# A sparse-attention decoder step: the samples' top-256 search as eight rows with halvings on ScalarE, and two prompt blocks halved on ScalarE alone

## The chip, the cores and the metric

The kernel runs on one core of a Trainium2 chip. The metric is the device time of one execution in microseconds (us); the time before is the median of three runs. A profile was taken of one further execution; its times are counted from the start of its span.

## The reference, cut to what matters

One layer of a hybrid decoder: a projection of the normalised input into many column groups, sparse attention on one branch, a causal pooling mixer on the other, and an output projection. The change touches the choice of the keys in the sparse attention. For every query the indexer gives a score per key, and only the 256 keys with the largest scores are attended to:

```python
s = jnp.einsum('bqhd,bld->bqhl', qi, ki)
score = jnp.einsum('bqh,bqhl->bql', wi, jax.nn.relu(s))
score = jnp.where(causal[None], score, -jnp.inf)
_, sel = lax.top_k(score, topk)          # topk = 256
```

The prompt has 1024 queries, in eight blocks of 128; blocks 0 and 1 have at most 256 keys and need no choice, block b has (b + 1) * 128 keys. There are eight sample sequences with one query each, over 1024 cached keys and the sample's own.

## The kernel before

The kernel keeps x transposed, makes the modulated input h as eight pairs of row tiles (an upper and a lower half, 16 tiles), and projects it for 21 column groups. A group's product goes in three chunks of 344 columns, 24 products of TensorE each (three for every k of 8). After every second k the function `project` calls `tick`, so a tick is six products, a chunk has four and a group twelve. Every other step of the kernel is a generator in a named queue, and a tick lets each queue's first generator go one step on, times its rate: a queue with rate 0.5 goes on at every second tick. TensorE, VectorE and ScalarE run their instructions in the order in which the code gives them out; so a side product whose input is late stops the projection behind it. GpSimd's order and the slots of tiles are left to the scheduler.

After the prompt's scores are made (`indexer`), 13 groups follow in the order u0 u1 u2 gp0 u3 gp1 q0 gp2 q1 gp3 q2 q3 ga3; ticks are counted here from the first product of u0 (184.19 us in the trace), so gp2 begins at tick 84. Beside them run:

- queue "smp", rate 1: `sample_indexer` (scores of the samples into s_sc, 128 partitions by 9 by 8: eight key slots and the own key, eight samples), then `sample_topk` from tick 49. It splits the scores into 16-bit halves and finds the 256th value by trying seven candidates at once, in twelve rounds: compare on VectorE (L968), count by nine products with ones on TensorE (`total`, L954, after five more ticks), choose on VectorE. Two more counts and a ranking of equal values follow, and the masks s_m.
- queue "top", rate TOP = 0.5: `topk` for the prompt's six blocks. Eight halvings of a threshold t by counting: blocks 7, 6, 5 by a Sign with accumulator on ScalarE (L758), 4, 3, 2 by a comparison with accumulator on VectorE (L761); then three tiny VectorE steps on all six (L764, L766, L768) make the next t, for which all six counts wait. Two steps (yields) a halving. After them those at or over t are marked (L773, L778), the at most 16 still missing are taken in two rounds of eight largest (L792) and replacement (L799); if that doesn't do, a branch runs 30 more rounds. The masks follow.
- queue "prep": among others `windows(g)` for the pooling group g, begun after u_g: GpSimd makes one to four running sums (L1187, with a copy of the edge columns, L1188), three ticks apart, VectorE's step follows (L1192 to L1197), then ScalarE casts the upper half pdh (L1201), GpSimd makes the lower half pdl (L1202) and TensorE turns the last columns (put, L1204). For g = 3 the first sum is given out at tick 61, VectorE's step at 73, the cast at 74.
- queue "pool": `take_gp` multiplies the pooled halves by w_pool on TensorE (ppo, L1217) for each chunk of gp_g; the last product of group 1 is given out at tick 75.
- queue "weights": the next group's weights, loaded two groups ahead, split one group ahead into an upper half on ScalarE (L293) and a lower half on GpSimd (L297), at the group's third tick.

Row tiles (up to 4 KB on each partition) come from one pool of 29. When group 3's first sum is given out, these 27 are taken: 16 of h, 5 of scores, up_out, pdh and pdl of groups 1 and 2, u3, and the sum itself would be one more, a second sum beside it the 29th.

Of the kernel before, what the change touches and what calls it, by code (L numbers as in the profile page):

```python
# [21 lines left out]
TOP = 0.5  # L22
# [8 lines left out]
LAG = 5  # L31
# [34 lines left out]
def kernel(  # L66
# [634 lines left out]
    def ordered_halves(hi, lo, src, sign):  # L701
        v = src.bitcast(I16).rearrange("p (n t) -> p n t", t=2)
        nc.vector.tensor_copy(hi, v[:, :, 1])
        nc.vector.tensor_copy(lo, v[:, :, 0].bitcast(U16))
        yield
        nc.vector.tensor_scalar(sign, hi, 0.0, -1.0, op0=ALU.is_lt, op1=ALU.mult)
        nc.vector.tensor_tensor(lo, lo, sign.bitcast(U16), op=ALU.bitwise_xor)
        yield
        nc.vector.scalar_tensor_tensor(hi, sign, 0x7FFF, hi, op0=ALU.bitwise_and, op1=ALU.bitwise_xor)

    TB = (7, 6, 5, 4, 3, 2)
    BY_ACT = (7, 6, 5)
    NT = len(TB)
# [12 lines left out]
    tk_flag = const.tile([P, NT], BF16, name="tk_flag")  # L726
    for i, b in enumerate(TB):
# [7 lines left out]
    def width(i):  # L735
        return (TB[i] + 1) * P

    def topk():
# [13 lines left out]
        nc.vector.tensor_tensor(t, t, tk_mv[:, :, 0], op=ALU.add)  # L752
        for k in range(HALVINGS):

            for i, b in enumerate(TB):
                L = width(i)
                if b in BY_ACT:
                    nc.scalar.activation(junk_tile("sg", tag="junka", bufs=1)[:, :L], score[b], AF.Sign, scale=-1.0,  # L758
                                         bias=t[:, i:i + 1], accum_out=cnt[:, i:i + 1])
                else:  # L760
                    nc.vector.tensor_scalar(junk_tile("junk")[:, :L], score[b], t[:, i:i + 1], None,  # L761
                                            op0=ALU.is_lt, op1=ALU.add, accum_out=cnt[:, i:i + 1])
            yield
            nc.vector.tensor_tensor(tk["keep"], cnt, tk["least"], op=ALU.is_le)  # L764

            nc.vector.scalar_tensor_tensor(tk["d"], tk["keep"], 0.5 if k < HALVINGS - 1 else 0.0, tk_step[:, k],  # L766
                                           op0=ALU.subtract, op1=ALU.mult)
            nc.vector.tensor_tensor(t, t, tk["d"], op=ALU.add)  # L768
            yield
# [32 lines left out]
        yield  # L802
        for r in range(WINDOW // 8):
# [3 lines left out]
            if r == 0:  # L807
                pb = ps_side("p_bad", (P, NT))
                mm(pb, ones_b, tk_flag, start=True, stop=True)
            those(r)  # L810
            if r == 0:
                yield
                with nc.allow_low_precision(reason="a count of at most 768"):
                    nc.vector.tensor_reduce(out=tk_bad, in_=pb[0:1, :], axis=AX.X, op=ALU.add)
# [3 lines left out]
        with tc.If(nc.vector.value_load(tk_bad) != 0, preferred_fallthrough_block=False):  # L818
            for r in range(WINDOW // 8, TOPK // 8):
# [44 lines left out]

    def s_bc(t):
        return t.unsqueeze(1).to_broadcast([P, 9, B])

    def sample_indexer():
# [54 lines left out]
        def weigh(b):  # L923
# [8 lines left out]
    steps = const.tile([P, 7, B], F32, name="steps")  # L932
    nc.gpsimd.iota(steps, pattern=[[1, 7], [0, B]], base=1, channel_multiplier=0,
                   allow_small_or_imprecise_dtypes=True)

    def sample_topk():
        s_hi = const.tile([P, 9 * B], I16, name="s_hi")
        s_lo = const.tile([P, 9 * B], U16, name="s_lo")
        s_sg = const.tile([P, 9 * B], I16, name="s_sg")
        nc.vector.tensor_scalar(s_sc, s_sc, 0.0, None, op0=ALU.add)  # L940
        yield from ordered_halves(s_hi, s_lo, s_sc.rearrange("p g b -> p (g b)"), s_sg)
        s_hi, s_lo = (t.rearrange("p (g b) -> p g b", b=B) for t in (s_hi, s_lo))
        s_H, s_low, s_ngt, s_least, s_need = (const.tile([P, B], F32, name=f"s_{n}")
                                              for n in ("H", "low", "ngt", "least", "need"))
        s_gt = const.tile([P, 9, B], BF16, name="s_gt")
        s_eq = const.tile([P, 9, B], BF16, name="s_eq")

        def total(flags, n):

            for _ in range(LAG):  # L950
                yield
            pt = ps_side("p_cnt", (P, n))
            for g in range(9):
                mm(pt, ones_b, flags[:, g], start=g == 0, stop=g == 8)  # L954
            yield
            return pt
# [806 lines left out]
```

## Time and profile before

| | us |
|---|---|
| time before, median of 3 runs (lowest to highest) | 648.01 (647.17 to 648.94) |
| the profiled execution | 648.84 |
| its span, first to last instruction | 647.1 |
| TensorE busy | 608.4 |
| VectorE busy | 403.9 |
| ScalarE busy | 291.1 |
| GpSimd busy | 256.9 |

TensorE is named PE in the rows, VectorE DVE, ScalarE ACT, GpSimd POOL. A busy time is the union of an engine's instructions; matmuls are pipelined and their ends are modelled, so 0.32 us of a product stands in the rows where the next one starts 0.16 us later. "PEclk" is the TensorE clock that was granted, as a share of the full one. Idle time is told with what ended it ("<- engine tile line"). Row lists by engine and time begin with start and duration in us.

### The profile page before, as it was taken

The page shows a single profiled execution, that of the slowest core. Times are in us where ns is not written, and L with a number is a line of the kernel's source. Part 1 is how long each engine was busy: PE and PEld are TensorE (multiplying, and loading weights), DVE is VectorE, ACT ScalarE, POOL GpSimd, SP SyncE. Part 2 cuts the span into 40 slices and gives each one's busy share as a digit, 9 for nine tenths or more (in the row PEclk, how much of TensorE's full clock was granted, in tenths as well). Part 3 has the DMA queues.
Part 4 walks back from the last instruction along what each step waited for, and adds up shares of the span by engine and source line. Part 5 has one row for each costly group of instructions (what it writes and reads, how often), then busy time and mean ns, then how long its engine had stood idle before and what let it go on. Part 6 is the DMA issues. An engine that isn't in the chain of part 4 may idle for free.

```text
span 647.1 us, 10990 instructions
## 1 busy us (share of the span) xinstructions
PE 608.4 (94%) x4197; PEld 500.5 (77%) x4197; DVE 403.9 (62%) x918; ACT 291.1 (45%) x518; POOL 256.9 (40%) x237
## 2 busy tenths in 40 slices
PE   5798998999989978979999988999999999999997
PEld 5587988999979868978988875656675666878876
DVE  4676364736467779997775546565687755554242
ACT  5634444444547865231222545755687544202000
POOL 3586434111267556552543690610445143106000
PEclk9999999999999988997999997999999999999999
DMA  8993115031245122121454250321221036146322
GB/s 304 297 291 61 50 44 152 16 84 55 76 128 147 34 66 56 44 58 44 99 135 138 89 164 26 138 99 33 66 67 34 1 99 220 43 151 209 98 97 68
DMA packets 75292, 66.05 MB, mean 102 GB/s; under 512 B 21828, under 2 KB 63900, under 8 KB 75229
## 3 DMA queue, kind: packets, MB, share of 16 engines
q1 hardware_dynamic: 69731, 50.57, 27.5%
q0 software_dynamic: 3008, 10.49, 5.3%
q10 hardware_dynamic: 2498, 4.27, 1.8%
q8 instruction: 33, 0.54, 0.3%
q14 instruction: 22, 0.18, 0.1%
HBM read 54.44 MB, written 11.10 MB: 101 GB/s over the span
## 4 chain that ended last, share of the span: by engine, by line
PE 74%; DVE 13%; ACT 5%; POOL 4%; DMA 2%; issue 2%; SPq 0%; POOLq 0%; ACTq 0%; DVEq 0%
PE py L1696 14%; PE po L1612 7%; PE pj_q L514 6%; PE pl L1575 6%; PE pT L1596 6%; PE pj_ga L514 5%; PE pj_qi L514 4%; PE pj_gp L514 4%; ACT sg L758 4%; PE pi L668 4%; PE pj_k L514 2%; PE pj_v L514 2%; DVE tk_t L768 2%; PE pj_u L514 2%; DMA vn<-in_cache_v_dram,pidx 1%
## 5 line engine op out<-in xcount | busy, mean ns | idle before, releaser
L1584 ACT ACTIVATE pr<-pr,mx,rq 128x128 f32<-128x128 f32 (+7 forms) x64 | 55.4, 866 | 18.2 <-DVE mx L1582 17.8
L677 DVE SCALAR_TENSOR_TENSOR sc<-r,wtok,sc 128x512 f32<-128x512 f32 (+5 forms) x42 | 44.1, 1060 | 27.9 <-ACT r L670 26.5
L670 ACT ACTIVATE r<-pi 128x512 f32<-128x512 f32 (+5 forms) x48 | 36.3, 759 | 54.1 <-PE pi L668 41.0
L1612 PE MATMUL po<-pTs,v_sb 128*64 128x256 f32 (+1 forms) x320 | 52.6, 381 | 0.0
L1696 PE MATMUL py<-woh,mh 128*128 128x512 f32 (+1 forms) x136 | 52.3, 384 | 0.0
L1696 PE MATMUL py<-woh,ml 128*128 128x512 f32 (+1 forms) x136 | 51.9, 382 | 0.0
L1696 PE MATMUL py<-wol,mh 128*128 128x512 f32 (+1 forms) x136 | 51.8, 381 | 0.0
L1596 PE MATMUL pT<-ident,pr 128*128 128x128 f32 x288 | 49.4, 285 | 0.1
L1578 DVE CUSTOM_DVE_ANT_0 pr<-pl,amask 128x384 f32<-128x384 f32 (+5 forms) x48 | 42.2, 887 | 10.9 <-PE pl L1575 10.5
L1596 PEld LDWEIGHTS pT<-ident,pr 128*128 128x128 f32 x288 | 33.0, 143 | 18.0 <-issue 15.8
L145 ACT COPY pTs<-pT 128x512 f32<-128x512 f32 x40 | 23.2, 581 | 34.6 <-PE pT L1596 34.6
L1716 DVE TENSOR_TENSOR y<-py,gate_p 128x512 f32<-128x512 f32 (+1 forms) x17 | 11.2, 657 | 43.0 <-PE py L1696 43.0
L1440 POOL TENSOR_TENSOR wol<-wo,woh 128x1024 fp32r<-128x1024 f32 x8 | 19.5, 2446 | 36.9 <-ACT woh L1439 30.6
L514 PE MATMUL pj_u<-hh,wh_u 128*128 128x344 f32 x96 | 32.5, 339 | 1.6 <-ACT r L670 1.6
L514 PE MATMUL pj_gp<-hh,wh_gp 128*128 128x344 f32 x96 | 33.5, 349 | 0.0
L514 PE MATMUL pj_q<-hh,wh_q 128*128 128x344 f32 x96 | 33.1, 345 | 0.0
L147 DVE COPY pTs<-pT 128x512 f32<-128x512 f32 (+1 forms) x40 | 23.3, 582 | 15.3 <-PE pT L1596 12.3
L514 PE MATMUL pj_gp<-hh,wl_gp 128*128 128x344 f32 x96 | 31.9, 332 | 0.0
L514 PE MATMUL pj_gp<-hl,wh_gp 128*128 128x344 f32 x96 | 31.8, 331 | 0.0
L514 PE MATMUL pj_q<-hl,wh_q 128*128 128x344 f32 x96 | 31.7, 330 | 0.0
L514 PE MATMUL pj_q<-hh,wl_q 128*128 128x344 f32 x96 | 31.6, 329 | 0.0
L1612 PEld LDWEIGHTS po<-pTs,v_sb 128*64 128x64 f32 x320 | 18.0, 135 | 17.4 <-issue 9.4
(451 smaller groups left out, 1780.3 us busy)
## 6 DMA issues: line engine op xcount, KB each, us to landing
ada<-in_w_ada_dram SPq DMA_DIRECT2D x16, 512.0 KB, 6.9
x<-in_x_prompt_dram SPq DMA_DIRECT2D x8, 512.0 KB, 5.4
gate<-in_w_ada_dram SPq DMA_DIRECT2D x8, 512.0 KB, 3.5
mix<-mix_dram SPq DMA_DIRECT2D x8, 512.0 KB, 3.1
xr<-in_x_prompt_dram SPq DMA_DIRECT2D x15, 256.0 KB
out_dram<-y ACTq DMA_DIRECT2D x15, 256.0 KB, 3.4
mix_dram<-sga SPq DMA_DIRECT2D x12, 172.0 KB, 4.9
mix_dram<-sgp SPq DMA_DIRECT2D x12, 172.0 KB, 2.8
```

Of the source, the lines that this page charges most:

```text
L147: nc.vector.tensor_copy(out, in_)
L514: mm(pt[:m, :n], wt[:, k, :m], ht[k][:, c0:c0 + n], start=k == 0 and q == 0, stop=k == KT - 1 and q == 2)
L668: mm(pt[:, c, :n], lhs, kk[:, l0:l0 + n], start=kk is kih, stop=kk is kil)
L670: nc.scalar.activation(r[:, 0:L].rearrange("p (c n) -> p c n", c=nh), pt[:, 0:nh, :n], AF.Relu)
L677: nc.vector.scalar_tensor_tensor(sb[:, 0:L], r[:, 0:L], wtok[:, b, h:h + 1], sb[:, 0:L], op0=ALU.mult, op1=ALU.add)
L758: nc.scalar.activation(junk_tile("sg", tag="junka", bufs=1)[:, :L], score[b], AF.Sign, scale=-1.0, bias=t[:, i:i + 1], accum_out=cnt[:, i: ...
L1575: mm(pt[:, c, :n], qst[j][s][:, b * P:(b + 1) * P], ksst[s][w][:, l0:l0 + n], start=w == 0, stop=w == 1)
L1578: nc.vector.tensor_tensor_reduce(out=pr[:, 0:L].rearrange("p (c n) -> p c n", c=nh), in0=pt[:, 0:nh, :n], in1=amask[b].rearrange("p (c n) ...
L1584: exps.append(lambda: nc.scalar.activation(pr[:, 0:L], pr[:, 0:L], AF.Exp, scale=sc, bias=mx, accum_out=sums[j, m][:, bq, s:s + 1]))
L1596: nc.tensor.transpose(pt[:, s, bq * P:(bq + 1) * P], probs[j, 2 * m + bq, s][:, k * P:(k + 1) * P], ident)
L1612: mm(po[j, m][64 * s:64 * s + 64, 0, q0:], v_sb[:, k, 64 * s:64 * s + 64], pTs[j, m, k][:, s, q0:], start=k == 0, stop=k == nk - 1)
L1696: mm(pt[:, part], a[k][:, bs], w[:, part], start=k == ks[0] and q == 0, stop=k == ks[-1] and q == 2)
```

## The change

It does four things. The samples' scores are turned into eight rows, one for each sample, of 1024 keys and the own one (`sample_search`, in place of `sample_topk`, `ordered_halves` and `total`): four transposes twice, mean and variance of the first 256 keys, eight halvings with three ScalarE instructions each (`half_way`: the Sign with accumulator, a Sign of the count against a limit, a new t), and two rounds of eight largest on VectorE (`sample_round`). Their masks are turned back by eight transposes (`sample_masks`), which the queue "top" now runs after the branch; the branch's flag counts the samples too, and `topk` waits with its own rounds until the queue "smp" is empty. Two row tiles are taken, s_row for the scores (until the masks) and s_fl for flags (until the marks). In the prompt's halvings blocks 7 and 6 go through `half_way`, so that no VectorE step lies between two of their counts; block 5 moves to VectorE, whose three tiny steps act on four blocks. A halving has three yields, and TOP is 0.6.

```diff
-TOP = 0.5
+TOP = 0.6
-LAG = 5
-    BY_ACT = (7, 6, 5)
-    NT = len(TB)
+    BY_ACT = (7, 6)
+    NT, NA = len(TB), len(BY_ACT)
+    def half_way(sc, t, cnt, lim, sign, step, junk):
+
+        nc.scalar.activation(junk, sc, AF.Sign, scale=-1.0, bias=t, accum_out=cnt)
+        nc.scalar.activation(sign, cnt, AF.Sign, scale=-1.0, bias=lim)
+        nc.scalar.activation(t, sign, AF.Identity, scale=step, bias=t)
...
+        for k in range(HALVINGS):
+            nc.gpsimd.tensor_scalar(tk_step[:, k, 0:NA], tk_step[:, k, 0:NA], 0.5, None, op0=ALU.mult)
...
+            for i in range(max(NA, NT - NA)):
+                if i < NA:
+                    half_way(score[TB[i]], t[:, i:i + 1], cnt[:, i:i + 1], tk_lim[:, i:i + 1], tk_sign[:, i:i + 1],
+                             tk_step[:, k, i:i + 1], junk_tile("sg", tag="junka", bufs=1)[:, :width(i)])
+                if i < NT - NA:
+                    o = NA + i
+                    nc.vector.tensor_scalar(junk_tile("junk")[:, :width(o)], score[TB[o]], t[:, o:o + 1], None,
+                                            op0=ALU.is_lt, op1=ALU.add, accum_out=cnt[:, o:o + 1])
+                if i % 2:
+                    yield
...
         chosen(0)
         yield
+        while queues["smp"]["gens"]:
+            yield
...
+                sample_round(r)
+        yield from sample_masks()
...
+    def sample_round(r):
+        sr = s_row["scores"]
+        sel, off, top = s_tk["sel"][:, 0:8], s_tk["off"][:, 0:8], s_tk["top"]
+        nc.vector.tensor_scalar(sel, tk_order[0:B, 0:8], 8.0 * r, s_tk["need"], op0=ALU.add, op1=ALU.is_lt)
+        nc.vector.tensor_scalar(off, sel, 1.0, -NEG, op0=ALU.subtract, op1=ALU.mult)
+        nc.vector.max(top, sr)
+        nc.vector.tensor_tensor(top, top, sel, op=ALU.mult)
+        nc.vector.tensor_tensor(top, top, off, op=ALU.add)
+        nc.vector.match_replace(sr, top, sr, NEG)
+
+    def sample_search():
+        sr = s_row["scores"] = row("s_row")[0:B, 0:S + 1]
+        fl = row("s_fl", BF16)[0:B, 0:S + 1]
...
+        for g in range(2):
+            pt = ps_side(f"p_row{g}", (B, 4, P))
+            for i in range(4):
+                nc.tensor.transpose(pt[:, i, :], s_sc[:, 4 * g + i, :], ident)
+            yield
+            nc.vector.tensor_scalar(by_slot(sr)[:, 4 * g:4 * g + 4, :], pt, 0.0, None, op0=ALU.add)
+            yield
...
+        nc.gpsimd.tensor_tensor(s_tk["sd"], s_tk["mv"][:, 1:2], tk["half"][0:B, 0:1], op=ALU.pow)
+        for k in range(HALVINGS):
+            nc.gpsimd.tensor_scalar(s_tk["step"][:, k:k + 1], s_tk["sd"], spans[7][1] * 2.0 ** -(k + 1), None, op0=ALU.mult)
+        nc.gpsimd.tensor_scalar(t, s_tk["sd"], spans[7][0], s_tk["mv"][:, 0:1], op0=ALU.mult, op1=ALU.add)
+        yield from lag(3)
+        for k in range(HALVINGS):
+            half_way(sr, t, s_tk["cnt"], s_tk["lim"], s_tk["sign"], s_tk["step"][:, k:k + 1], fl)
+            yield
+            yield
+        nc.vector.tensor_tensor(t, t, s_tk["step"][:, HALVINGS - 1:], op=ALU.add)
+        nc.vector.tensor_scalar(fl, sr, t, None, op0=ALU.is_ge, op1=ALU.add, accum_out=ngt)
+        yield
+        nc.vector.tensor_scalar(d, ngt, float(TOPK), NEG, op0=ALU.is_lt, op1=ALU.mult)
+        nc.vector.scalar_tensor_tensor(sr, fl, d, sr, op0=ALU.mult, op1=ALU.add)
...
+        for r in range(WINDOW // 8):
+            yield
+            sample_round(r)
+
+    def sample_masks():
...
+        yield from lag(2)
+        pt = ps_side("p_smask", (P, 8, B))
+        for i in range(8):
+            nc.tensor.transpose(pt[:, i, :], by_slot(sr)[:, i, :], ident[0:B, 0:B])
+        yield
+        nc.vector.tensor_copy(s_m[:, 0:8, :], pt)
+        yield
...
-    beside("smp", sample_topk(), 1.0)
+    beside("smp", sample_search(), 1.0)
...
-    drain("prep", "pool", "top", "smp", "stack")
+    drain("prep", "pool", "smp", "top", "stack")
```

## Rows read from the trace of the kernel before

**Rows 1.** The page: the chain that ended last, share of the span by engine.

```profile
PE 74%; DVE 13%; ACT 5%; POOL 4%; DMA 2%; issue 2%; SPq 0%; POOLq 0%; ACTq 0%; DVEq 0%
```

**Rows 2.** Stretches: us; busy PE, PEld, DVE, ACT, POOL (instructions); PEclk; DMA share; GB/s.

```profile
184.00:253.00 69.00, 62.49 (x421) 56.93 (x422) 52.33 (x140) 45.17 (x85) 44.71 (x44) 0.95 0.35 98
253.00:300.00 47.00, 41.01 (x277) 39.60 (x276) 44.06 (x76) 10.92 (x21) 25.07 (x17) 0.93 0.22 55
300.00:385.00 85.00, 85.00 (x670) 77.35 (x669) 54.82 (x127) 29.33 (x54) 47.72 (x26) 1.00 0.41 116
385.00:400.00 15.00, 10.89 (x48) 7.33 (x45) 7.95 (x36) 7.64 (x19) 4.22 (x3) 0.66 0.05 18
```

**Rows 3.** What PE waited for: us in total, times, longest us.

```profile
PE p_cnt L954 <- DVE s_fl L968: 5.9, 3, 4.2
...
PE p_ix L911 <- ACT kidT L905: 2.5, 3, 1.7
PE p_ixT L920 <- DVE rx L925: 2.3, 3, 1.9
...
PE put L1204 <- ACT pt L1220: 1.4, 1, 1.4
```

**Rows 4.** The chain in order of time, some PE pieces: start, us, what.

```profile
188.74 0.11 PE pvts L1084
...
299.84 1.89 PE pj_gp L514 x12
301.72 0.22 PE p_cnt L954 x9
```

**Rows 5.** Groups of DVE, 253 to 385 us: busy, mean ns; idle before.

```profile
L799 DVE MATCH_REPLACE8 sc<-tk_top,sc 128x1024 f32<-128x1024 f32 (+5 forms) x12 | 10.4, 874 | 0.0
L792 DVE MAX8 tk_top<-sc 128x8 f32<-128x1024 f32 (+5 forms) x12 | 10.2, 882 | 0.0
L976 DVE SCALAR_TENSOR_TENSOR s_H<-s_d,s_H 128x8 f32<-128x8 f32 x6 | 7.0, 1170 | 0.2
```

**Rows 6.** Groups of ACT, 186 to 385 us, with what ended the idle time.

```profile
L758 ACT ACTIVATE sg<-sc,tk_t 128x1024 bf16<-128x1024 f32 (+2 forms) x24 | 25.0, 1043 | 9.5 <-DVE tk_t L768 8.2 <-DVE ps L1192 0.7
...
L758 ACT ACTIVATION_READ_ACCUMULATOR sg<-sc,tk_t 128x1 f32 x24 | 4.5, 187 | 0.0
...
L1509 ACT COPY ev_g<-pa_g 128x256 f32<-128x256 f32 x3 | 1.1, 372 | 7.1 <-PE pa_g L1506 5.7 <-issue 1.4
L1514 ACT COPY gate_s<-pg 9x256 f32<-9x256 f32 x3 | 1.1, 362 | 4.7 <-PE pg L1512 4.7
```

**Rows 7.** Groups of DVE, 184 to 253 us.

```profile
L768 DVE TENSOR_TENSOR tk_t<-tk_t,tk_d 128x6 f32<-128x6 f32 x8 | 11.0, 1377 | 0.3
L1195 DVE SCALAR_TENSOR_TENSOR ps<-ps,u 128x1031 f32<-128x1031 f32 (+2 forms) x3 | 3.7, 1231 | 0.0
```

**Rows 8.** DVE in order of time, 186 to 260 us.

```profile
221.27 0.87 DVE L761 TENSOR_SCALAR_CACHE_REDUCE junk<-sc,tk_t 128x640 bf16<-128x640 f32 x1
...
236.31 6.43 DVE L768 TENSOR_TENSOR tk_t<-tk_t,tk_d 128x6 f32<-128x6 f32 x1
...
252.66 2.27 DVE L940 TENSOR_SCALAR s_sc<-s_sc 128x72 f32<-128x72 f32 x1
```

**Rows 9.** POOL in order of time, 186 to 385 us.

```profile
220.90 2.39 POOL L297 TENSOR_TENSOR wl_gp<-wr_gp,wh_gp 128x1024 fp32r<-128x1024 f32 x1
...
236.63 1.90 POOL L1187 TENSOR_TENSOR ps<-u 128x1023 f32<-128x1023 f32 x1
...
265.79 2.41 POOL L1187 TENSOR_TENSOR ps<-u 128x1023 f32<-128x1023 f32 x1 [7.56 <-ACT u L1021]
...
278.23 0.19 POOL L1188 COPY ps<-ps 128x8 f32<-128x8 f32 x1
```

**Rows 10.** ACT in order of time, 186 to 385 us.

```profile
286.56 1.04 ACT L293 CAST wh_gp<-wr_gp 128x1024 fp32r<-128x1024 f32 x1
...
289.07 0.55 ACT L1269 ACTIVATE qp<-pj_q,vT 128x344 f32<-128x344 f32 x1 [1.02 <-POOL pdl L1202]
```

More of the change, by code (lines that the diff above doesn't have):

```diff
@@ L726 @@
     tk_flag = const.tile([P, NT], BF16, name="tk_flag")
+    tk_lim = const.tile([P, NA], F32, name="tk_lim")
+    tk_sign = const.tile([P, NA], F32, name="tk_sign")
+    for i in range(NA):
+        nc.gpsimd.memset(tk_lim[:, i:i + 1], (TB[i] + 1) * P - 2 * TOPK + 0.5)
     for i, b in enumerate(TB):
@@ L807, in topk @@
             if r == 0:
-                pb = ps_side("p_bad", (P, NT))
-                mm(pb, ones_b, tk_flag, start=True, stop=True)
+                pb = ps_side("p_bad", (P, NT + 1))
+                mm(pb[:, 0:NT], ones_b, tk_flag, start=True, stop=True)
+                mm(pb[:, NT:], ones_b[0:B, :], s_tk["flag"], start=True, stop=True)
             those(r)
@@ L812, in topk @@
                 yield
-                with nc.allow_low_precision(reason="a count of at most 768"):
+                with nc.allow_low_precision(reason="a count of at most 776"):
                     nc.vector.tensor_reduce(out=tk_bad, in_=pb[0:1, :], axis=AX.X, op=ALU.add)
@@ new lines @@
+    s_row = {}
+    s_tk = {n: const.tile([B, k], BF16 if n == "flag" else F32, name=f"s_{n}")
+            for n, k in (("t", 1), ("cnt", 1), ("lim", 1), ("sign", 1), ("sd", 1), ("step", HALVINGS), ("mv", 2), ("ngt", 1),
+                         ("d", 1), ("need", 1), ("flag", 1), ("sel", 16), ("off", 16), ("top", 8), ("self", B))}
+    nc.gpsimd.memset(s_tk["lim"], S + 1 - 2 * TOPK + 0.5)
+    nc.gpsimd.tensor_scalar(s_tk["self"], ident[0:B, 0:B], 1.0, -MASKED, op0=ALU.subtract, op1=ALU.mult)
@@ L999, in sample_topk @@
             yield
-        p_rk = ps_side("p_rk", (P, 2, B))
-        mm(p_rk[:, 0, :], tri, s_row, start=True, stop=True)
-        mm(p_rk[:, 1, :], ones_b, s_row, start=True, stop=True)
+        st = small.tile([P, 6], F32, tag="tk_st", name="s_st")[0:B]
+        nc.vector.bn_stats(st, sr[:, 0:2 * P])
+        nc.vector.bn_aggr(s_tk["mv"], st)
         yield
-        nc.vector.tensor_tensor(s_m[:, 0, :], p_rk[:, 0, :], s_eq[:, 0, :], op=ALU.add)
-        for t in range(1, 8):
-            nc.vector.tensor_tensor(s_m[:, t, :], s_m[:, t - 1, :], s_eq[:, t, :], op=ALU.add)
@@ new lines, in sample_search @@
+        nc.vector.scalar_tensor_tensor(sr, fl, d, sr, op0=ALU.mult, op1=ALU.add)
+        yield
+        nc.vector.tensor_scalar(d, ngt, float(TOPK), -1.0, op0=ALU.is_lt, op1=ALU.mult)
+        nc.vector.tensor_scalar(need, d, ngt, float(TOPK), op0=ALU.mult, op1=ALU.add)
+        nc.vector.tensor_scalar(s_tk["flag"], need, float(WINDOW), None, op0=ALU.is_gt)
+        for r in range(WINDOW // 8):
+            yield
+            sample_round(r)
+    def sample_masks():
+        sr = s_row["scores"]
+        nc.vector.tensor_scalar(sr, sr, TAKEN, MASKED, op0=ALU.is_gt, op1=ALU.mult)
+        nc.vector.scalar_tensor_tensor(s_m[0:B, 8, :], ident[0:B, 0:B], sr[:, S:S + 1], s_tk["self"], op0=ALU.mult, op1=ALU.add)
+        yield from lag(2)
[5 more added lines that the diff above has]
+        yield
```

100 lines of the change are left out of this document (11 added, 89 removed).

## Prediction

> **What bounds the kernel now.** I read the chain of waits first, then the busy time by stage, then what TensorE waits for, then VectorE, ScalarE and GpSimd in the stages that the change touches. The chain lies on TensorE for 74% of the span [rows 1]: TensorE is the bound, and another engine matters only where it makes TensorE wait or lose clock. The table by stage says where that is [rows 2]. In stage A, 184 to 253 us (the prompt's halvings beside the projections), TensorE is idle for 69.00 - 62.49 = 6.5 us, and at a granted clock of 0.95 up to 3.5 us more of full speed are missing. In B, 253 to 300 us (the samples' old search begins), it is idle for 6.0 us, with 0.07 x 47 = 3.3 us of clock missing. In C, 300 to 385 us, it has no idle time and full clock. In D, 385 to 400 us, 4.1 us are idle at a clock of 0.66; that wait is for the last projection's norms, which the change leaves alone. So the change can win some 10 us in A, 9.3 in B, and in C only what it takes off TensorE itself.
>
> The gaps have names [rows 3]. In A, TensorE's side products wait 2.5 us for a ScalarE copy (kidT) queued behind Sign counts, 2.3 us for a VectorE step (rx) queued behind others, and 1.4 us for a bank that ScalarE empties late. In B it waits 5.9 us, 4.2 of them at once, for the comparison flags of the samples' search: all but 0.1 us of B's idle time.
>
> **Part 1: the samples' old search goes.** It puts 14 counts of nine small products and two for the ranks on TensorE, 0.22 us a count [rows 4]: five fall in B (1.1 us), nine in C (2.0 us). B's waits are for its flags, so B's 6.0 idle and 3.3 clock go: -9.3 us, if nothing else is late there. On VectorE it frees much: one group of six [128x8] steps alone shows 7.0 us [rows 5], most of it holding. That is not on the path once the waits are gone.
>
> **Part 2: the new search.** TensorE gets eight 8-row transposes in B and eight into masks in C; the nearest row, one 128-to-8 transpose, is 0.11 us [rows 4], so 0.9 us each time (bounds for the masks, whose moving side is 8 wide, 0.2 and 0.9). VectorE gets two rounds; a largest is 0.88 and a replacement 0.87 in the mean of widths from 384 to 1024 [rows 5], at 1025 wide some 1.2, with five tiny steps at 0.2 some 3.4 us a round, 6.8 together, and about 6 us for the copies, the count and the masks. In C TensorE has waited for no VectorE step, so I cost these 13 us at nothing; without that cover they would still be less than what part 1 takes off. The eight halvings go to ScalarE. Rows do not shorten with partitions: 9x256 takes 362 ns, 128x256 takes 372 [rows 6]. So a Sign over 8 rows of 1025 costs what a block of 1024 does: the mean row of 1043 ns [rows 6] is that of widths 1024, 896 and 768, so about 1.15, and 0.19 for the accumulator's read. The two [8x1] steps cost between 0.19 (that read) and 0.36 each [rows 6]; I take 0.27, the middle. That is 1.9 us a halving, 15 us in all, in 16 ticks (17 us of TensorE's products). ScalarE's other work there is 10.92 us in 47 [rows 2], so 4 in 17: it ends some 2 us behind (4 at the dear end), which four projection banks cover; uncovered it is those 2 to 4 us.
>
> **Part 3: blocks 7 and 6 on ScalarE alone, 5 on VectorE.** Eight halvings cost ScalarE 24 Signs now (25.0 + 4.5 us, 3.7 a halving) [rows 6]; afterwards a halving is two Signs of 1.34 and 1.23 and four tiny steps, 3.65. The size stays, but a wait goes: ScalarE stood 8.2 us before Signs for VectorE's new threshold [rows 6]. VectorE gets block 5: from the 640-wide count of 0.87 [rows 8], 768 wide is 1.0 us, 8 us in all. It is busy for 52.33 us of A [rows 2] and would be for 60, with A 59 long at full gain. Its threshold step takes 1377 ns in the mean [rows 7] and 6.43 us once, while GpSimd runs its sums from 236.63 [rows 8, 9]; this holding stays, and VectorE steps behind it still feed TensorE. A halving gets 3/0.6 = 5 ticks in place of 2/0.5 = 4, which gives both engines more room. So A's gain lies between 0 and 10, and I take half, -5: of [rows 3] the ScalarE waits lose their cause, the VectorE ones don't. GpSimd gets eight small scalings before the halvings and ten small steps before the samples'. It is busy for 44.71 of 69 us in A and 25.07 of 47 in B [rows 2], so nothing; uncovered 18 x 0.36 (the dear tiny row) = 6.5 us.
>
> The Trainium skill speaks against the move of block 5: its GPSIMD Engine Reference (Specifications) says that GpSimd's SBUF interfaces are shared with VectorE, and that Vector instructions in a two-port mode or with two SBUF inputs contend. By that rule a one-input count could be held too, and eight more counts held as long as the threshold step would cost A its whole gain (the 648 of rival 2). The trace holds the two-input step and one plain one-input step (2.27 us for 72 columns at 252.66), but the count at 221.27 ran in 0.87 us beside GpSimd's 2.39 us [rows 8, 9].
>
> **Part 4: two more row tiles, and the running sums of group 3.** The new s_row and s_fl come from the pool of 29 row tiles. Counted from the code, the samples' search starts at tick 49 of this stage, as the old one did; s_fl is last used at tick 74, s_row when the masks are made. When the first running sum of group 3 (windows) is given out at tick 61, 27 tiles are taken, as the section on the kernel lists them. With the new two it is 29, so this sum has no slot. Next to come free are group 1's pooled halves, after the last gp1 product with them on TensorE, tick 75; s_fl comes free behind the VectorE step of windows itself (tick 73) and cannot help. That such waits exist shows at 289.07, where ScalarE waits 1.02 us for an unrelated GpSimd step before it may write qp [rows 10].
> What follows is worked out from that product, P. GpSimd: 0.5 to start and 4 x (1.90 + 0.19) (a sum and its edge copy [rows 9]): P + 8.9. VectorE's step: 1.23 [rows 7] and three tiny ones: P + 10.5. VectorE stands in that wait from tick 73, with the samples' and the top-k steps queued behind it. ScalarE stands at the cast after it, and the cast of the next weights, wh_gp2, is queued behind: two casts of 1.04 [rows 10], P + 12.6. GpSimd then makes the pooled lower half and wl_gp2, 2.39 each by a step of that size [rows 9]: from P + 11.5 to P + 16.3. TensorE needs both at tick 84: 54 products at 1.89/12 [rows 4] and P's own three, P + 9.0, and has 0.3 us of work between the two waits. So it stands for 7.0 us. The earlier stands lost 3.3 us of clock (6.0 idle, B) and up to 5.1 us (0.34 x 15, D) [rows 2]; I take 3.4. Together +10.4 in B. If a slot is found after all it is 0.
>
> **Sum**, against the profiled execution's own 648.84 us (span 647.1, 1.7 around it), which lies 0.8 us above the median of 648.01: A -5.0; B -9.3 - 1.1 + 0.9 + 10.4 = +0.9; C -2.0 + 0.9 = -1.1; in all -5.2, so 643.6 from the profiled time and 642.8 from the median. I take 643.
>
> **Rivals.**
> 1. The running sum finds a slot in time, or its wait is covered: without the 10.4 us, 643 - 10.4 = 632.6. For: the pool was full before without a stall of that size. Against: the count by name. 0.22.
> 2. Stage A gains nothing, since VectorE, now with four counts, takes ScalarE's place as what the side products wait for: 643 + 5 = 648. For: 60 us of work for 59. Against: five ticks where there were four, and no wait of ScalarE for VectorE. If counts are held (the rule above), it ends here. 0.18.
> 3. The other side, slower: VectorE and GpSimd hold each other. Before, group 3's four sums took 12.6 us (265.79 to 278.42, 2.41 us for the first [rows 9], with a weight split between them) and not 8.4. Then TensorE stands 4.2 us longer and loses the 5.1 us of clock, +5.9, and the same holding takes A's 5: 643 + 5.9 + 5 = 654. It decides from about 7 us of extra holding (650). For: the 6.43 us step. Against: VectorE stands still in that very wait and cannot hold GpSimd there. 0.13.
> 4. The change doesn't do what it says: a sample's halvings end more than 16 short, and the branch of 30 rounds runs, at some 10 us a round (half of 10.4 + 10.2 [rows 5]) 300 us more, near 945. Worked out on the reference's inputs, the eight searches end 1 to 6 short of 256. 0.01.
>
> **How the numbers follow.** The forecast has 0.46 (its own spread is 640 to 646, from the ends of clock and A). The range takes in rivals 1 and 2 and most of the way to rival 3: 632 to 652. About 0.3% (1.9 us) is what a measurement can tell from no change. Faster: the forecast and rival 1, 0.68; same: rival 2, 0.18; slower: rivals 3 and 4, 0.14.
>
> **What would show it.** The flag counts gone from TensorE's waits. In their place one wait of near 7 us, of the gp2 products for wh_gp2 or wl_gp2, with group 3's sums on GpSimd starting right behind a gp1 product with the pooled halves and not behind u3's copy, and VectorE idle before windows' step; if the sums start right behind u3, part 4 is wrong and the time is near 632. In A, Signs without waits for a VectorE threshold; if TensorE's gaps at the samples' indexer still sum to 6 us, rival 2 holds. The samples' Signs near 1.34 us with their read at 8 rows, and counts of 768 at 1.0 us, not 2.4. The prediction fails as a whole if C, free of idle time before, shows waits.

## The result, and the profile of the changed kernel

The change makes the kernel slower: 654.59 us in the median of five executions (652.80 to 655.37) against 648.01 (645.86 to 649.61, five executions beside it) before, a ratio of 1.0102 with a 95% interval of 1.0082 to 1.0123. The forecast was 643, its range 632 to 652. The profiled execution took 655.37 us, with a span of 653.6.

The chain of waits by engine (the row that answers to [rows 1]) shows that TensorE lost part of it: 69% in place of 74%.

```profile
PE 69%; DVE 10%; POOL 6%; DMA 5%; ACT 4%; issue 3%; SPq 2%; POOLq 0%; DVEq 0%; ACTq 0%
```

The same stretches as in [rows 2]: busy us of PE, PEld, DVE, ACT, POOL, then the granted clock.

```profile
184.00:253.00 69.00, 62.36 (x427) 56.98 (x428) 58.05 (x148) 48.57 (x102) 48.52 (x51) 0.95 0.36 98
253.00:300.00 47.00, 38.23 (x233) 37.14 (x230) 26.47 (x52) 23.84 (x51) 25.21 (x27) 0.94 0.15 39
300.00:385.00 85.00, 79.80 (x549) 72.69 (x550) 46.26 (x91) 26.63 (x50) 43.05 (x22) 0.95 0.39 108
```

A has as much TensorE work as before. B has less busy time, although the waits for the flag counts are gone from it. C, which had no idle time and full clock, now has 5.2 us of the one and a clock of 0.95. What TensorE waits for (it answers to [rows 3]):

```profile
PE ppo L1214 <- DVE rx L931: 4.2, 1, 4.2
PE pj_gp L513 <- POOL wl_gp L296: 4.0, 1, 4.0
...
PE pqt L1253 <- DVE tk_bad L821: 3.9, 1, 3.9
PE ppo L1214 <- ACT pt L1217: 3.3, 1, 3.3
PE pj_gp L513 <- ACT wh_gp L292: 2.7, 1, 2.7
...
PE put L1201 <- DVE rx L931: 1.1, 1, 1.1
```

Six waits, 19.2 us, where before four kinds made 12.1 in these stages. For comparing kernels, three sections between products serve better than fixed times: A from the first product of u0 to the last of u3, B on to the first of gp2, C on to the last of ga3. They come from rows like these, of the changed kernel (duration in ns, first and last start in us):

```profile
L513 PE MATMUL pj_u<-hh,wh_u x96: 313/320/537, 185.4 to 264.0; 128*128 128x344 f32 x96
...
L513 PE MATMUL pj_gp<-hh,wh_gp x48: 313/321/636, 296.6 to 348.5; 128*128 128x344 f32 x48
...
L513 PE MATMUL pj_ga<-hh,wh_ga x24: 313/320/431, 377.8 to 391.2; 128*128 128x344 f32 x24
```

So A takes 264.0 - 185.4 = 78.6 us, B 32.6, C 94.6; before they took 80.4, 35.1 and 84.5. A and B won 4.3 us, C lost 10.1, and u0 began 1.2 us later (in the kernels below it begins between 183.9 and 186.4). The sum of these is +7.0; the span grew by 6.5. A section comes from the one profiled execution of a kernel, and these lie up to 2.0 us off their kernel's median (before 648.84 for 647.1 in the runs beside e1, e12 636.62 for 638.60, e10 642.51 for 640.67). So less than some 2 us between two sections can't be told from no difference.

**What happens from 283 us on.** GpSimd in order of time:

```profile
283.16 0.93 POOL L1219 TENSOR_TENSOR sgp<-sgp,pt 128x344 f32<-128x344 f32 x1 [3.59 <-ACT pt L1217]
284.04 1.89 POOL L1184 TENSOR_TENSOR ps<-u 128x1023 f32<-128x1023 f32 x1
...
290.34 2.41 POOL L1184 TENSOR_TENSOR ps<-ps 128x1016 f32<-128x1016 f32 x1
...
295.55 2.38 POOL L1199 TENSOR_TENSOR pdl<-ps,pdh 128x1032 fp32r<-128x1032 f32 x1 [2.66 <-ACT pdh L1198]
297.89 3.32 POOL L296 TENSOR_TENSOR wl_gp<-wr_gp,wh_gp 128x1024 fp32r<-128x1024 f32 x1
```

Group 3's first sum begins at 284.04, right behind the last gp1 product (283.13 to 283.9 on TensorE) and 13 us after ScalarE's last copy of u3 (270.77). That is the row-tile wait of part 4. VectorE in the same time:

```profile
290.30 0.17 DVE L1189 TENSOR_TENSOR ps<-hsum,u 128x8 f32<-128x8 f32 x1 [16.53 <-POOL ps L1185]
...
295.89 3.11 DVE L989 SCALAR_TENSOR_TENSOR s_row<-s_fl,s_d,s_row 8x1025 f32<-8x1025 bf16 x1
...
299.52 1.71 DVE L952 TENSOR_SCALAR s_sel<-tk_order,s_need 8x8 f32<-8x8 f32 x1
...
303.27 1.19 DVE L955 TENSOR_TENSOR s_top<-s_top,s_sel 8x8 f32<-8x8 f32 x1
...
305.89 0.21 DVE L952 TENSOR_SCALAR s_sel<-tk_order,s_need 8x8 f32<-8x8 f32 x1
...
307.46 0.16 DVE L955 TENSOR_TENSOR s_top<-s_top,s_sel 8x8 f32<-8x8 f32 x1
...
309.05 4.84 DVE L796 MAX8 tk_top<-sc 128x8 f32<-128x1024 f32 x6
...
314.44 0.42 DVE L1249 COPY qs<-pqs 128x256 f32<-128x256 f32 x1
```

VectorE stands for 16.5 us and, after one small step, 2.5 more; then it works without a gap for 21.5 us, and only behind that comes qs, the copy of the squared norms of query group 0, for which TensorE waits 3.9 us. The samples' count, marks and two rounds (294.2 to 309.0) and the prompt's first six MAX8 are all ahead of it. Part of that time is no work: the first round took 6.4 us and the second, with the same steps, 3.2, since the first ran beside GpSimd's large steps (wl_gp, sgp, wl_q). By my estimate some 5 us of the 21.5 are such holding: 1.0 us of the 1.19 and 1.5 of the 1.71 above, against the same lines in the second round, 0.7 for a step at 301.26, and 1.8 of the 3.11 against the 1.28 of a like step over 128x1024 at 261.22. That is more than the 3.9 us that TensorE waits. ScalarE's halvings of the samples:

```profile
266.85 1.16 ACT L733 ACTIVATE s_fl<-s_row,s_t 8x1025 bf16<-8x1025 f32 x1 [5.50 <-POOL s_t L979]
...
278.46 1.14 ACT L733 ACTIVATE s_fl<-s_row,s_t 8x1025 bf16<-8x1025 f32 x1
279.51 0.18 ACT L733 ACTIVATION_READ_ACCUMULATOR s_fl<-s_row,s_t 8x1 f32 x1
279.72 0.29 ACT L734 ACTIVATE s_sign<-s_cnt,s_lim 8x1 f32<-8x1 f32 x1
280.05 0.39 ACT L735 ACTIVATE s_t<-s_sign,s_t,s_step 8x1 f32<-8x1 f32 x1
```

One halving is 1.9 us (278.46 to 280.34). The first began only at 266.85, for which ScalarE had waited 5.50 us: VectorE's copies of the rows and then GpSimd's ten small steps (263.1 to 266.8) came before it.

### The profile page after: what moved, and what is told of

It reads as the page before. It is cut to its first block, busy times and chain, and to the rows that moved or that the text cites. A ratio compares the mean times of both kernels' runs of the same rounds, so it can differ in the third digit from the quotient of the medians.

```text
span 653.6 us, 10781 instructions
## 1 busy us (share of the span) xinstructions
PE 607.0 (93%) x4086; PEld 499.6 (76%) x4086; DVE 384.9 (59%) x872; ACT 307.2 (47%) x566; POOL 262.9 (40%) x258
## 4 chain that ended last, share of the span: by engine, by line
PE 69%; DVE 10%; POOL 6%; DMA 5%; ACT 4%; issue 3%; SPq 2%; POOLq 0%; DVEq 0%; ACTq 0%
PE py L1693 14%; PE po L1609 7%; PE pT L1593 6%; PE pl L1572 6%; PE pj_ga L513 5%; PE pj_q L513 5%; PE pj_qi L513 4%; PE pj_gp L513 4%; PE pi L667 4%; DVE junk L763 2%; PE pj_k L513 2%; PE pj_v L513 2%; PE pj_u L513 2%; DMA ada<-in_w_ada_dram 2%; DVE tk_keep L767 1%
## 5 line engine op out<-in xcount | busy, mean ns | idle before, releaser
L1575 DVE CUSTOM_DVE_ANT_0 pr<-pl,amask 128x384 f32<-128x384 f32 (+5 forms) x48 | 42.2, 887 | 10.4 <-PE pl L1572 10.0
L146 DVE COPY pTs<-pT 128x512 f32<-128x512 f32 (+1 forms) x40 | 23.3, 583 | 15.4 <-PE pT L1593 12.7
```

Source lines behind the costliest of these rows:

```text
L146: nc.vector.tensor_copy(out, in_)
L1575: nc.vector.tensor_tensor_reduce(out=pr[:, 0:L].rearrange("p (c n) -> p c n", c=nh), in0=pt[:, 0:nh, :n], in1=amask[b].rearrange("p (c n) ...
```

## The experiments

Each kernel was run in five rounds beside the kernel before, whose median lay between 646.4 and 647.1 in these runs. Sections A, B, C are read as above.

| kernel | us | ratio to before (95%) | A | B | C |
|---|---|---|---|---|---|
| before | 648.01 | | 80.4 | 35.1 | 84.5 |
| after | 654.59 | 1.010 (1.008 to 1.012) | 78.6 | 32.6 | 94.6 |
| e1_own_tiles | 647.10 | 1.000 (0.998 to 1.002) | 78.6 | 26.8 | 92.1 |
| e2_two_rows_held | 654.50 | 1.011 (1.008 to 1.015) | 80.2 | 41.5 | 84.5 |
| e3_prompt_alone | 645.81 | 0.998 (0.995 to 1.000) | 76.5 | 36.1 | 84.5 |
| e4_samples_alone | 651.07 | 1.007 (1.005 to 1.009) | 80.8 | 29.2 | 93.4 |
| e5_eights_later | 639.09 | 0.987 (0.983 to 0.990) | 78.6 | 26.8 | 84.7 |
| e6_rounds_later | 639.83 | 0.989 (0.985 to 0.992) | 78.4 | 27.0 | 83.7 |
| e7_short_eights_later | 648.48 | 1.000 (0.998 to 1.003) | 79.1 | 29.9 | 89.9 |
| e9_samples_own_tiles | 644.49 | 0.996 (0.994 to 0.999) | 78.2 | 25.4 | 90.6 |
| e8_samples_eights_later | 642.58 | 0.994 (0.991 to 0.997) | 78.2 | 25.4 | 84.6 |
| e10_block5_on_scalar | 640.67 | 0.990 (0.987 to 0.994) | 81.7 | 25.5 | 84.8 |
| e11_steps_accumulate | 642.59 | 0.995 (0.993 to 0.997) | 82.5 | 25.4 | 84.7 |
| e12_samples_share_06 | 638.60 | 0.988 (0.985 to 0.991) | 79.4 | 24.7 | 82.9 |

### Is it the row tiles? e1 and e2

e1_own_tiles takes the two tiles out of the pool:

```diff
-        sr = s_row["scores"] = row("s_row")[0:B, 0:S + 1]
-        fl = row("s_fl", BF16)[0:B, 0:S + 1]
+        sr = s_row["scores"] = amask_all[0:B, 0:2 * S + 2].bitcast(F32)
...
+                     junk_tile("sg", tag="junka", bufs=1, n=S + 1)[0:B])
...
+        fl = junk_tile("s_fl", n=S + 1)[0:B]
```

> The changed kernel with its two new row tiles taken out of the row pool: s_row lies in the memory of the top-k masks, which are written only after its last reading, and the Signs' flags go to ScalarE's scratch tile. Nothing else differs from the changed kernel. Theory 1 (row shortage): the 9.1 and 9.0 us that ScalarE and VectorE stand around pdh go, gp2 no longer waits (6.8 us of TensorE) and the VectorE backlog in front of qs (3.9 us of TensorE) goes with it, with some 2 to 3 us of low clock: 640 to 644 us, that is 10 to 14 below the changed kernel and below the old one. Theory 2 (contention): the backlog is VectorE's own work held by GpSimd; freed of the stand it stays late elsewhere, TensorE's waits move to pt, rx and put: 650 to 655 us.

Measured: 647.10 us. (VectorE's stand, which the expectation put at 9 us, is 16.5 in the row above.) Both waits of gp2 are gone, as theory 1 says, but the time misses its range by 3 us: it stops at that of the old kernel, 7.5 below the changed one, and TensorE now waits longer at qs:

```profile
PE pqt L1257 <- DVE tk_bad L824: 7.1, 1, 7.1
PE ppo L1218 <- DVE rx L934: 4.2, 1, 4.2
```

B has its whole gain (26.8 for 35.1), C loses 7.6 of it again. So the shortage explains the difference to before in number, and hides a second loss of the same size. VectorE ahead of the wait, in e1_own_tiles:

```profile
284.62 0.15 DVE L988 TENSOR_TENSOR s_t<-s_t,s_step 8x1 f32<-8x1 f32 x1 [0.51 <-ACT s_t L738]
...
294.01 2.33 DVE L959 TENSOR_TENSOR s_top<-s_top,s_off 8x8 f32<-8x8 f32 x1
...
299.90 0.15 DVE L959 TENSOR_TENSOR s_top<-s_top,s_off 8x8 f32<-8x8 f32 x1
...
301.29 4.84 DVE L799 MAX8 tk_top<-sc 128x8 f32<-128x1024 f32 x6
306.17 0.21 DVE L802 TENSOR_TENSOR tk_top<-tk_top,tk_sel 128x48 f32<-128x48 f32 x1
306.41 0.21 DVE L803 TENSOR_TENSOR tk_top<-tk_top,tk_off 128x48 f32<-128x48 f32 x1
306.71 0.43 DVE L1253 COPY qs<-pqs 128x256 f32<-128x256 f32 x1
```

No stand is left, and VectorE is busy for 45.15 of the 47 us from 253 to 300. It waits 0.51 us for ScalarE's last halving and then works for 22.1 us up to qs. Some 7 of these are holding, estimated as above (the step at 294.01 took 2.33 us, its like at 299.90 took 0.15). So theory 2's contention has a share in this backlog, though its time (650 to 655) was not reached; no run here takes the holding away from it.

e2_two_rows_held does the reverse, on the old kernel:

```diff
+        held = [row(f"held{i}")[0:B, 0:1] for i in range(2)]
+        for h in held:
+            nc.vector.memset(h, 0.0)
...
+        nc.vector.tensor_tensor(held[0], held[0], held[1], op=ALU.add)
```

> The old kernel with two further tiles of the row pool held from the first to the last step of its sample_topk (written by two memsets of 8 elements, read by one addition of 8 elements at the end); nothing else differs. Theory 1 (row shortage): the sums of group 3 stand until the last gp1 product, wh_gp2 and wl_gp2 come late, TensorE stands some 7 us there and some 3 to 4 more at qs, with a lower clock: 656 to 662 us. Theory 2 (contention of the new steps): the old kernel has room to work off the stand, at most 3 us: 648 to 651 us.

Measured: 654.50 us, 7.4 above before, a little under the range of theory 1. The trace of e2_two_rows_held names the releaser of group 3's first sum, a product of gp1, and what TensorE waits for:

```profile
282.58 1.89 POOL L1191 TENSOR_TENSOR ps<-u 128x1023 f32<-128x1023 f32 x1 [3.89 <-PE ppo L1221]
```
```profile
PE p_cnt L957 <- DVE s_fl L971: 12.8, 1, 12.8
```

So two tiles held are enough for the stand, without any other part of the change. In the old one the stand shows at another place, the flags of the samples' search, since they are queued behind windows' step on VectorE.

### The two halves by themselves: e3 and e4

e3_prompt_alone is the old kernel with the halvings of the diff and TOP = 0.6; e4_samples_alone is the changed kernel with them undone (BY_ACT of 7, 6, 5; TOP = 0.5).

> The old kernel with the prompt's half of the change alone (blocks 7 and 6 halved on ScalarE alone, block 5 counted on VectorE, share 0.6); the samples' search is the old one with its counts on TensorE. By the prediction's step for stage A: 5 us less, 643. By the theory formed from the trace after (VectorE full in stage A, its two-input steps still held by GpSimd for up to 5 us, so that the waits only move from pix to ppo and put): within 2 us of the old kernel, 646 to 650.

> The changed kernel with the prompt's half undone (blocks 7, 6 and 5 counted on ScalarE, their steps on VectorE, share 0.5); the samples' rows, halvings and rounds of eight largest are the new ones, with the two row tiles. Theory 1 (row shortage): it has the whole loss, 652 to 657 us. Rival (the prompt's half, by block 5's 8 us on VectorE, is what made the backlog): it is faster than the old kernel by the 9 us of the counts' waits less the stand, 640 to 646 us.

Measured: 645.81 us for the prompt's half, 1.3 us less than before in the runs beside it and just under the theory's range; the 5 us of the prediction's step are not there (in the profiled runs A is shorter by 3.9, of which B gives back 1.0). The samples' half takes 651.07, a little under the range given: gp2's two waits sum to 8.3 us and qs waits 3.1, but A keeps its old waits. The rival for e4 falls. The halves don't add up: the samples' half alone loses 3.9 us against the 647.14 beside it, and the prompt's half, which alone wins 1.3, adds 654.59 - 651.07 = 3.5 on top of it.

### Is it the order on VectorE? e5, e6 and e7

In the changed kernel the prompt's rounds wait until the queue "smp" is empty, which is at tick 77; qs is given out at tick 88. e5_eights_later, the kernel of e1 otherwise, lets them begin some 12 ticks later:

```diff
         while queues["smp"]["gens"]:
             yield
+        yield from lag(7)
```

> The kernel of e1_own_tiles, with the prompt's rounds of eight largest begun seven yields (some 12 ticks) later, behind the copy qs of query group 0 instead of ahead of it. Nothing is left out. Theory (order on VectorE): in e1_own_tiles the six MAX8 of 4.8 us and the two tiny steps behind them, emitted in the ticks just before qs, are the last part of the backlog for which TensorE waits 7.1 us there; that wait falls to about 1.7 us and some 1.5 us of low clock go too: 639 to 642 us. Rival (VectorE is full as such, the work only moves): a wait of the same size appears later, at the next qs or at the scores' end, 645 to 648 us.

e6_rounds_later does it by beginning the samples' steps after the halvings 16 ticks later, and e7_short_eights_later is e5's edit on the changed kernel with its row shortage.

> The kernel of e1_own_tiles, with the samples' steps after their halvings (s_t's addition, the count, the marking, the two rounds of eight largest, which take 16 us on VectorE there) begun 16 ticks later, behind qs; the prompt's eight largest follow them as before. Nothing is left out. Theory (order on VectorE): nothing but the windows' step stands ahead of qs, the wait of 7.1 us is gone, C is free of idle as in the old kernel: 637 to 640 us. Rival (VectorE full): 645 to 648 us.

> The changed kernel (row tiles from the pool) with only the prompt's eight largest begun seven yields later, behind qs. Theory: the stand at gp2 (6.8 us) stays, the wait of 3.9 us at qs and the low clock that follows it go: 648 to 651 us, so that the changed kernel's 7.5 us above e1_own_tiles are the gp2 stand alone. Rival: the wait at qs stays since the windows' step and the samples' rounds are still ahead of it: 653 to 655 us.

Measured: 639.09, 639.83 and 648.48 us, each within its range for the order. In e5_eights_later the wait at qs is what was left of it by the expectation:

```profile
PE pqt L1258 <- DVE qs L1254: 1.7, 1, 1.7
```

C is back at 84.7. VectorE does the same work in another order and nothing returns later, so it was not full there, only asked in the wrong order. e6 has no wait at qs at all, but 5.6 us in place of 4.1 behind the last product; its last masks are written at 369.5, and whether they are the reason no run shows. The four kernels give each loss twice: the order costs 647.10 - 639.09 = 8.0 us without the shortage and 654.59 - 648.48 = 6.1 with it; the shortage costs 654.59 - 647.10 = 7.5 with the bad order and 648.48 - 639.09 = 9.4 without.

### What the prompt's half is worth: e9, e8 and e12

e9_samples_own_tiles is e4_samples_alone with e1's edit, e8_samples_eights_later adds e5's (six yields at a share of 0.5), e12_samples_share_06 raises the share behind that point (and has seven yields again):

```diff
+        queues["top"]["gens"] = [(g, 0.6) for g, _ in queues["top"]["gens"]]
```

> The kernel of e4_samples_alone (the samples' half of the change alone) with the two row tiles out of the row pool, as in e1_own_tiles. Theory 1 (row shortage): its two waits at gp2 (8.3 us) go, and VectorE, which has not the 8 us of block 5's counts here, is less behind at qs: 640 to 643 us. Rival: the waits move to qs as they did in e1_own_tiles, 645 to 648 us.

> The kernel of e9_samples_own_tiles (the samples' half alone, own tiles), with the prompt's eight largest begun six yields (12 ticks at its share of 0.5) later, behind qs. Nothing is left out. Beside e5_eights_later it differs by the prompt's half of the change alone. Theory (order on VectorE): the wait of 5.6 us at qs falls under 2 us, 637 to 640 us, so the prompt's half is worth nothing there, since VectorE's 8 us more in stage A take back what the Signs' waits gave. Rival (the prompt's half is worth the 3.9 us that stage A showed in e3_prompt_alone): 642 to 643 us.

> The kernel of e8_samples_eights_later (the samples' half alone, own tiles, eight largest behind qs) with the share of the prompt's top-k raised from 0.5 to 0.6 at that point, so that its last masks are written about as early as in e5_eights_later. Nothing is left out. It differs from e5_eights_later by the prompt's halvings alone. Theory (the 3.5 us by which e8_samples_eights_later lay above e5_eights_later are its wait of 7.7 us in place of 4.1 behind the last product, because the masks came late): that wait is back at about 4 us, 637 to 639.5 us, and the prompt's half of the change is worth nothing beside the new samples' half. Rival (the 3.5 us are the prompt's half): 641 to 643 us.

Measured: 644.49 for e9, between the two theories: gp2's waits are gone, but qs waits 5.6 us. 642.58 for e8, in the range of the rival. But its A and B are no longer than those of e5 and its wait at qs fell to 1.7; what grew is a wait behind the last product, in e8_samples_eights_later, and it is back to its size in e12_samples_share_06:

```profile
PE p_sl L1296 <- DVE qbd L1259: 7.7, 1, 7.7
```
```profile
PE p_sl L1297 <- DVE qbd L1260: 4.3, 1, 4.3
```

At a share of 0.5 the prompt's masks were still being written at 359 to 371 us. (The last link of this wait is GpSimd's step for the norms, 4.2 us, which begins at 378.48 in e8 and at 375.77 in e5; how the late masks hold it up the traces don't name.) With 0.6 e12 comes to 638.60, e5's time within what can be told. So beside the new samples' search the prompt's half is worth nothing that can be told: it takes ScalarE's waits from A and puts VectorE's in their place.

### What fills stage A: e10 and e11

e10_block5_on_scalar gives block 5 to ScalarE as well (BY_ACT of 7, 6, 5 in e5, same ticks). e11_steps_accumulate writes e5's three threshold steps as twelve in the accumulating form, for each block o, such as

```diff
...
-            nc.vector.tensor_tensor(t[:, by_dve], t[:, by_dve], tk["d"][:, by_dve], op=ALU.add)
+                nc.vector.tensor_scalar(tk_scr[:, 0:1], tk["d"][:, o:o + 1], t[:, o:o + 1], None,
+                                        op0=ALU.add, op1=ALU.add, accum_out=t[:, o:o + 1])
```

> The kernel of e5_eights_later with the prompt's block 5 halved on ScalarE too (eight Signs of 768 columns and sixteen tiny steps, some 13 us more on ScalarE; eight counts, 8.7 us, less on VectorE), at the same ticks. Nothing is left out. Theory 3 (stage A's wait of 4.2 us for rx and 1.3 for put comes from a full VectorE): they go, 634 to 637 us. Rival (they come from the two-input steps that GpSimd's runs hold for 5.2 us, wherever the counts are): the wait stays at 3 us or more, 638 to 641 us. Rival (ScalarE, with 62 of 69 us, becomes the bound): new waits for kidT or pt, 640 to 644 us.

> The kernel of e5_eights_later with the three two-input steps of a VectorE halving (keep, d, t over four blocks) written as twelve counts of one or two columns in the accumulating form, which the trace of before shows at their plain length beside GpSimd's sums. Nothing is left out. Theory 4 (hold): no step takes more than 0.3 us, the twelve take about 2.8 us a halving in place of 2.4 on average, and the one delay of 5.2 us that makes rx late is gone: the wait for rx falls to under 2 us, 636 to 638 us. Rival (fullness): VectorE's sum in stage A is no smaller, the wait stays or grows, 639 to 642 us.

Measured: 640.67 and 642.59 us, 1.6 and 3.5 above e5, with A longer by 3.1 and 3.9. In e10 the 4.2 us for rx are gone, but ScalarE, busy for 56.7 of 69 us, makes new waits (its second rival), and put still waits 2.3 us for rx:

```profile
PE p_ix L921 <- ACT kidT L915: 5.2, 2, 3.6
```

That doesn't yet speak for theory 3, since the long hold went too: the longest step of a halving is 5.28 us in e5_eights_later (at 233.99) and 2.34 in e10_block5_on_scalar:

```profile
246.92 2.34 DVE L772 SCALAR_TENSOR_TENSOR tk_d<-tk_keep,tk_step 128x3 f32<-128x3 f32 x1
```

In e11 none of the steps is held: of one kind the shortest, the median and the longest are 214, 215 and 219 ns, with a read of the accumulator behind each, and the other two kinds are like it. But all of them together are longer:

```profile
L779 DVE TENSOR_SCALAR_CACHE_REDUCE tk_scr<-tk_two,tk_step x28: 214/215/219, 201.1 to 248.1; 128x2 f32<-128x2 f32 x28
L779 DVE DVE_READ_ACCUMULATOR tk_scr<-tk_two,tk_step x28: 82/83/86, 201.3 to 248.3; 128x1 f32 x28
```
```profile
PE put L1214 <- DVE rx L943: 4.7, 1, 4.7
```

Twelve times 215 + 83 ns is 3.6 us a halving, more than the 2.8 I expected and than the 2.4 of the held form. The wait for rx at ppo falls from 4.2 to 1.1 us, and TensorE waits at put instead. With the long hold gone, as in e10, that wait is gone or short, so the held step made most of it. That the sum of VectorE's work bounds A is not shown: over all of A VectorE was busy for 69.7 of 78.6 us in e5 and 71.5 of 82.5 in e11, so the sum grew by 1.8 us and A by 3.9, with 11 us of idle time on VectorE. Less work on VectorE (e10) and no held step (e11) each left A longer than it was in e5. Whether a form that is neither held nor longer would bring A's last 3 us was not tried.

## Why the prediction was wrong

- **Part 4, the row tiles: right.** The sums stand until P, gp1's last product (283.13). From there the text gave P + 8.9 for the sums (measured P + 9.8; its 0.5 us to start comes from no row, and the start took 0.9), P + 12.6 for wh_gp2 (P + 13.5) and P + 16.3 for wl_gp2 (P + 18.1, since wl_gp took 3.32 us and not 2.39). TensorE stands 2.72 + 4.05 = 6.8 us there, by the text 7.0. That this agrees so well is in part luck: GpSimd was 1.8 us later than in the text, and TensorE reached the wait 1.8 us later too (P + 10.8 for P + 9.0), as its products ran at the low clock for a while. The whole item was +10.4; it measures 7.5 and 9.4.
- **Part 2, "In C TensorE has waited for no VectorE step, so I cost these 13 us at nothing": this step failed.** Without this loss the change would have been level with before (e7, a ratio of 1.000), still not faster, as A falls short too. That C was free of idle time says that the work then queued on VectorE was early enough. It doesn't say how much more fits ahead of a given copy. In the old kernel the MAX8 ran from 281.8 to 294.5 between the samples' counts, and qs came at 304.5 behind an idle time of VectorE. In the new one `while queues["smp"]["gens"]` moves the prompt's rounds behind the samples', and both are given out in ticks 73 to 87, right ahead of qs at 88, on an engine already behind. The text names the steps "queued behind" VectorE's stand and stops there, without asking who waits for that queue. It also has a round at 3.4 us, which is right for the second (3.2) and not for the first, held one (6.4). Price: 6.1 us in the changed kernel, 8.0 without the shortage. The text's last test, that it fails as a whole if C shows waits, is what the trace shows.
- **Stage A, -5.0: wrong**, -1.8 measured, and not even that is shown to be the halvings' work: with the old halvings A lies between 78.2 and 80.8 us (before, e2, e4, e8, e9, e12). The ScalarE waits did lose their cause: ScalarE no longer waits 8.2 us for a new threshold [rows 6], and kidT is gone from TensorE's list. But rx takes their place, 5.2 us with put where A had 6.2. VectorE is busy for 58 of 69 us, and a step held beside GpSimd delays rx:

```profile
235.91 5.29 DVE L767 TENSOR_TENSOR tk_keep<-tk_cnt,tk_least 128x4 f32<-128x4 f32 x1
```

  VectorE in ScalarE's place is what rival 2 says, given 0.18. It has VectorE full (60 us of work for 59); here the held step makes the longest wait, and that fullness as such does it is not shown. The text's "this holding stays" was right; what it would cost was not worked out. The terms for VectorE's work were right: eight counts of 768 columns took 8.1 us, 1008 ns each.
- **Stage B, -9.3 - 1.1 + 0.9: right but for a little.** Without the shortage B is shorter by 8.3 (e1, e5), with 1.4 us of it left in a wait of ppo for pt. The text has a halving right (1.9 us), though two tiny steps at 0.54 us together, and they take 0.29 + 0.39. What it put at nothing is GpSimd's ten small steps: they took 3.7 us ahead of the first halving, for which ScalarE waited 5.50 us (2.80 in e7, the same kernel up to there, and 3.16 in e1). VectorE's first step on s_row had also waited 1.42 us for its row tile, at 253.60. So ScalarE ran later than the text has it. The text also said that four projection banks cover the lag, but pt empties one of two banks for side products: in the changed kernel that costs 3.3 us once (0.6 in e7; in e1 it is 1.4, and there pt itself waits 0.85 us for a GpSimd step).
- **Stage C, -2.0 + 0.9: not contradicted once qs is out of the way**: 83.7 in e6 and 82.9 in e12 for 84.5, but 84.7 in e5, where qs still waits 1.7 us.
- **Rivals.** Rival 1 (a slot is found) was run as e1_own_tiles: 647.1, not 632.6. The misses in A and C sat in the base of the sum, so its time was as wrong as the forecast's. Rival 3 has the measured time, 654, but not by its mechanism: the four sums took 8.85 us, not 12.6. The holding that it names did take part, on VectorE's side: some 5 us of the steps ahead of qs.

Against the forecast of 643 the terms are, from medians and from sections of single executions: order on VectorE +6.1, A +3.2, C +1.3 (0.2 in e5 for -1.1), B +1.2, the later start of the profiled run +1.2, the shortage 9.4 for 10.4, -1.0. Together +12.0; measured +11.6.

Of the versions run, e5_eights_later (the whole change) and e12_samples_share_06 (its samples' half) are 1.2 to 1.4% faster than the old kernel and 2.4% faster than the changed one. A gain of 8 us is there once the two tiles leave the pool and the rounds are given out behind qs. That is about half of the 15.4 that the text's sum gives without the shortage (648.0 to 632.6).

## What to carry to other kernels

When steps are added to an engine that runs in the order given, look for the next instruction in its queue that the bound engine waits for, and count all that is now given out ahead of it, stands included; that an engine caused no wait before says nothing about the room it has. Tiles from a shared pool are a resource with a count: two more of 29 held here cost 7 to 9 us, in a place that has nothing to do with their use. And take both losses away before judging either: here removing one gave back exactly the old time, which looked like a change that does nothing.

## What the runs showed of the hardware

- Which VectorE instructions GpSimd's work holds goes by their form and width. A two-input step over 4 columns was held for 5.29 us while GpSimd ran three large steps back to back (235.09 to 241.2), and a plain one-input step over 8 columns took 1.71, up to the end of GpSimd's wl_gp. Three plain one-input steps over one column, just before it and beside the same wl_gp (299.04 to 299.59), took 0.14 to 0.20. The accumulating form is not held: the 32 counts of stage A ran within 0.02 us of one another at each of their four widths, and the one- and two-column steps of e11 took at most 219 ns among the same sums. The Trainium skill's GPSIMD Engine Reference (Specifications) says that Vector instructions in a two-port mode or with two SBUF inputs contend; by that rule the two-input steps are held and these counts need not be, and the traces agree. In which mode a plain one-input step ran no trace here shows.
- The clock lost in a stand is not back with the next product. In the changed kernel the granted clock, the mean of its two levels over a stretch, is below full in all four stretches from 283 us to 325, and TensorE has no idle time in the last of them, from 315 to 325:

```profile
283.00:293.00 10.00, 9.87 (x53) 9.87 (x54) 0.24 (x2) 2.23 (x6) 9.49 (x9) 0.83 0.10 26
293.00:303.00 10.00, 3.23 (x14) 2.66 (x14) 9.75 (x14) 6.11 (x11) 7.45 (x4) 0.76 0.03 8
303.00:315.00 12.00, 8.06 (x58) 7.34 (x57) 11.62 (x24) 1.01 (x2) 2.38 (x2) 0.92 0.46 116
315.00:325.00 10.00, 10.00 (x55) 10.00 (x56) 8.42 (x22) 2.40 (x4) 6.27 (x3) 0.83 0.05 18
```

  The products show what these means are made of:

```profile
286.15 0.49 PE L513 MATMUL pj_q<-hh,wl_q 128*128 128x344 f32 x1
286.44 0.49 PE L513 MATMUL pj_q<-hh,wh_q 128*128 128x344 f32 x1
...
288.56 0.32 PE L513 MATMUL pj_q<-hh,wh_q 128*128 128x344 f32 x1
288.72 0.32 PE L513 MATMUL pj_q<-hl,wh_q 128*128 128x344 f32 x1
```

  TensorE had idled for 3.27 us before 283.13. Its products then start 0.16 us apart at first, 0.29 apart from 284.7 to 287.9 (the lower level, 1.2 GHz), and 0.16 apart again (2.4 GHz). Behind the stands that end at 301.26 and at 314.92 they are 0.29 apart up to 304.9 and 318.4. Each time 11 to 12 products took some 0.13 us more, about 1.5 us in all, which comes on top of the stand. So it is three short spells and not one long one. e5_eights_later, whose only wait there is 1.7 us, has 1.00 in all four stretches.
- A ScalarE step over one column is not as short as the reading of an accumulator: 0.29 us for a Sign and 0.39 for the form with scale and bias from memory, against 0.18 for the read.
